# The chunk recurrence of an S5 branch: eight chunks at a time on the DVE, and the context's scan as a tree

## The chip, the cores and the metric

The kernel runs on one core of one Trainium2 chip. The metric is the time of one execution on the device in microseconds (us). The engines are named as in the profile: PE is the matrix engine (PEld its weight loads), DVE the vector engine, ACT the scalar engine, POOL (here also "the Pool") a second vector-like engine, SP the engine that issues the loads from HBM.

## The reference: what is computed

Two layers of a model with 512 latent tokens and 256 context tokens of 1024 features, all in float32. Each layer projects its normed tokens and feeds three mixers side by side, attention, a short convolution and a state space (S5), gates and sums the three, projects, and then runs an MLP:

```python
zx = xn @ w_in
att_x = merge_heads(blocked_attend(q_x, k_all, v_all)) @ w_o
conv_x = short_conv(...)
s5_x, s5_h = s5_branch(zh_s5, zx[..., OFF_S5:OFF_G], a_re, a_im, ...)
y = (g[:, :, 0] * y_att + g[:, :, 1] * y_conv + g[:, :, 2] * y_s5) @ w_out
```

The S5 branch has 32 groups of 64 complex states, in two directions (the latent tokens follow the context in each). For each state it is the recurrence `s[t] = A s[t-1] + B u[t]` over the 768 tokens, and the output is a product of the states with C. The second layer needs the context's outputs no more, only the state at its end.

## The kernel before

The matmuls are exact to float32 in three passes: a block of weights comes by an SP load (tile `wr`), ACT rounds it to `wh` (L175), the DVE subtracts for `wl` (L176; the Pool does it in layer 1's first gate stage, `LOP`), and PE multiplies high by high and high by low (L265) and low by high (L271). A list of steps sets in which order the blocks are emitted, with a look-ahead for the loads and the splits. Other work is put in as a generator: after some of the steps `bg.step()` advances it to its next `yield`. A scheduler that plans the instructions on a time line then decides each engine's final order.

S5 goes by chunks of eight tokens: 32 chunks of the context and 64 latent ones. PE computes each chunk's own contribution to the state at its end (the drive) into the tile `W`, 128 partitions (64 states of two directions) by 2 (real, imaginary), 32 groups and 96 chunks; the chunks are innermost, so the 64 numbers of one chunk lie 384 bytes apart. Then `recur` (L1268) runs `W[s] += A^8 W[s-1]` over the chunks, four TENSOR_TENSORs of 64 elements for each: L1286 and L1288 multiply by the real and the imaginary part of `A^8` (tile `arec`), L1287 and L1289 add. In layer 0 steps 1 to 30 are on the DVE and 31 to 95 on the Pool (`RCUT`); in layer 1, which has the context's end state from elsewhere, the 64 latent steps are on the DVE. Its `yield`s are doled out in the gate stages: `gate` (L1310) multiplies by the gate's weights and ACT takes the sigmoid `sg` (L1314), `merge` (L1320) forms `m` from `sg` and the product (L1324, then L1326 and L1327). The first gate stage (attention's gate) goes with the recurrence; in the second (the convolution's) the readout begins, once the recurrence has been drained: `read_load` copies the states of a quarter of the groups, shifted by a chunk, into `so` (ACT L1385, DVE L1383 and L1386), and `read_mm` multiplies them by a table `ct` (L1401).

In layer 1 the context's 32 chunks are run through by `early_scan` (L1202) during attention, in two halves of 16 groups: 31 steps of four Pool instructions of 32 elements each (L1207 to L1210). Slabs are tiles of 768 numbers a partition, from one ring of 40 that nearly all activations share.

Of the kernel before, what the change touches and what calls it, by code (L numbers as in the profile page):

```python
# [10 lines left out]
F32 = mybir.dt.float32  # L11
# [3 lines left out]
OP = mybir.AluOpType  # L15
# [10 lines left out]
G = 32  # L26
CH = 16
T = 8
# [11 lines left out]
RCUT = (30, 95)  # L40
RSTEP = 6
# [30 lines left out]
def hybrid_kernel(ctx: ExitStack, tc: tile.TileContext, x, c, ctx_in, c_ctx, ada_w, ada_b, norm_mix, w_in,  # L72
# [30 lines left out]
    def load(dst, src):  # L103
        """a load; the first ones go in the order in which they are given."""
        ins = nc.sync.dma_start(dst, src)
        if order[0]:
            tc.keep_in_program_order(ins)
# [55 lines left out]
    class Weights:  # L163
        """A block of weights: loaded, then split into hi and lo."""
# [13 lines left out]
        def cols(self, o, stride, nk):  # L178
            """the k tiles [128, 128] from column o on, hi and lo."""
            return [[w[:, o + k * stride:o + k * stride + 128] for k in range(nk)] for w in (self.hi, self.lo)]  # L180

    def block(src):
        """src [nk * 128, ncol] -> [128, nk, ncol]"""
# [42 lines left out]
    class Background:  # L226
        """Work that is emitted in small steps between the blocks of the main stream."""
# [20 lines left out]
    def staged(items, *stages):  # L248
        """item i goes through stage s in step i + s."""
# [23 lines left out]
    def mm3(ps, w, ah, al, sg, o=0):  # L273
        """ps[:, s:e] = sum_k W[k]^T a[k] with W = wh + wl, a = ah + al."""
# [23 lines left out]
    def ada_mm(i, st):  # L298
        """four column tiles of the array work side by side."""
# [26 lines left out]
    def rsqrt_(ss, n, scale):  # L326
        """returns 1 / sqrt(ss * scale + eps), [128, n] (Newton from an integer estimate)."""
# [10 lines left out]
    def col_stats(acc, s, e, scale):  # L338
        """sums of acc[:, s:e] over partitions -> 1 / rms, tokens on the partitions."""
# [14 lines left out]
    def modulate(l, w, X, rb, segments, xh, xl, ks=range(KD), lag=MLAG):  # L354
        """xn[:, s:e] = rms(x) * norm * (1 + scale) + shift, split; segments: (s, e, which vectors)."""
# [37 lines left out]
    arec = [cst.tile([128, 2, 2, G], F32, name=f"arec{l}") for l in range(2)]  # L393

    def s5_prep(l):
# [4 lines left out]
        def inputs(g8):  # L400
            """B and C of eight groups."""
# [40 lines left out]
        def weave(*chains):  # L442
            """chains of small instructions that don't depend on each other, side by side."""
# [61 lines left out]
        def signs():  # L505
            """sn = s_ * n2 + c_ * u_ with the sign q; cs = c_ * n2 + s_ * u_ with the sign m_."""
# [44 lines left out]
        def factor():  # L551
            """f = (A - 1) / a"""
# [18 lines left out]
        # powers by slot: A^(s + 1) and A^(8 - s) for C, A^s and A^(7 - s) for B (forward, backward)  # L571
# [31 lines left out]
        def tables(u, st):  # L603
            """C A^k and A^k B for two groups."""
# [110 lines left out]
    def kv_part(k):  # L715
        """k tile k of the first two blocks, for all tokens."""
# [30 lines left out]
    def rot_cols(v, o):  # L747
        """columns o..o+32 of v [128, k, n] are pe; the next 32 become rot(pe)."""
# [6 lines left out]
    def roped(d, t):  # L755
        """rows 64-95 of d, lat: pe * cos + rot * sin, with rot in the rows 96-127."""
# [4 lines left out]
    def first_blocks(blocks, SEG, xargs, done):  # L761
        """The first two blocks after a norm: the tokens of SEG[0] go first, while SEG[1] is still being normed.

        xargs: (layer, which norm, the sums); done[i](ps) takes the product of block i."""
# [32 lines left out]
    def layer(l):  # L797
# [68 lines left out]
        # keys' rotary part  # L866
# [24 lines left out]
        # S5 inputs, to [(T - 1 - i, ch), group, chunk]  # L891
# [125 lines left out]
        def scores(h, half, kts):  # L1017
            """exp(s - max) and its sums, 256 queries (which come scaled)."""
# [19 lines left out]
        def turned(kts, P):  # L1038
            """P^T, split: pairs of key tiles side by side."""
# [660 lines left out]
```

## Time and profile before

| | |
|---|---|
| runs | 2454.41, 2459.8, 2459.3 us; median 2459.3 |
| profiled execution | span 2455.2 us |
| busy | PE 96%, DVE 55%, ACT 36%, POOL 21% of the span |
| layer 0: chunk recurrence | on the DVE from 475.4 us, on the Pool to 623.5 |
| layer 0: first readout on PE | 621.9 us |
| layer 1: chunk recurrence | on the DVE, last instruction at 1891.8 us |
| layer 1: first readout on PE | 1896.8 us |

Times are positions in the span of the profiled execution, which is 4.1 us shorter than the median. A line of a group names the code line, the engine, the operation, output and inputs by tile, the shape (partitions x elements) and the count; then busy time and mean duration, then idle time of the engine before these instructions and what ended it. A line of waits says who waited (engine, tile, line) for whom, in total, how often, and the longest.

### The profile page before, as it was taken

What the parts mean: (1) busy time and instruction counts of PE and PEld (TensorE: products, weight loads), DVE (VectorE), ACT (ScalarE), POOL (GpSimd) and SP (SyncE); (2) the same over time, 40 slices, a digit from 0 to 9 for tenths busy, and PEclk for the clock granted to TensorE, in tenths of its full rate; (3) what the DMA queues carried; (4) which work ended last, traced back from release to release, by engine and by line L of the source; (5) the groups of instructions that cost most, each with busy time, mean ns of one, the idle gap of its engine ahead of it and who ended that gap; (6) DMA issues with size and microseconds to landing.
All of it is one profiled execution on the core that took longest, in us unless ns stands there. A gap on an engine that the chain in (4) does not pass through costs nothing. (4 is left out here: it accounts for less than half of the span.)

```text
span 2455.2 us, 36706 instructions
## 1 busy us (share of the span) xinstructions
PE 2364.2 (96%) x14326; PEld 1989.0 (81%) x14326; DVE 1352.6 (55%) x2577; ACT 887.3 (36%) x1520; POOL 516.1 (21%) x906
## 2 busy tenths in 40 slices
PE   5889999999899999999999999999998999999998
PEld 3778888888788888888888888888776788888887
DVE  6985456743322466666533337566678435644455
ACT  5545345412242342332222215455531433432222
POOL 3561111069101110222300001217750010100000
PEclk7999999999999999999999999999998999999999
DMA  9544443421442223455533214333451834333331
GB/s 294 135 115 119 124 133 108 129 87 50 143 143 61 61 85 109 123 149 167 147 120 93 67 54 139 71 97 79 127 160 53 247 99 122 93 95 97 100 96 52
DMA packets 410049, 278.76 MB, mean 114 GB/s; under 512 B 77476, under 2 KB 401236, under 8 KB 409876
## 3 DMA queue, kind: packets, MB, share of 16 engines
q1 hardware_dynamic: 409876, 276.41, 39.2%
q8 instruction: 113, 1.85, 0.3%
q14 instruction: 60, 0.49, 0.1%
HBM read 239.92 MB, written 36.44 MB: 113 GB/s over the span
## 5 line engine op out<-in xcount | busy, mean ns | idle before, releaser
L175 ACT ACTIVATE wh<-wr 128x1024 fp32r<-128x1024 f32 (+1 forms) x294 | 292.7, 999 | 492.8 <-PE psA L271 278.8
L176 DVE TENSOR_TENSOR wl<-wr,wh 128x1024 fp32r<-128x1024 f32 (+1 forms) x281 | 329.4, 1175 | 210.3 <-ACT wh L175 209.0
L265 PE MATMUL psA<-xh,wh 128*128 128x512 f32 (+1 forms) x1312 | 347.0, 342 | 4.9 <-DVE zr L823 3.5
L265 PE MATMUL psA<-xh,wl 128*128 128x256 f32 (+1 forms) x1312 | 344.3, 340 | 0.0
L271 PE MATMUL psA<-xl,wh 128*128 128x256 f32 (+1 forms) x1312 | 243.8, 337 | 0.0
L265 PEld LDWEIGHTS psA<-xh,wh 128*128 128x128 f32 x1312 | 205.4, 190 | 37.3 <-ACT xh L364 3.9
L265 PE MATMUL psB<-xh,wl 128*128 128x512 f32 (+1 forms) x576 | 225.1, 391 | 6.4 <-DVE wl L176 6.4
L265 PE MATMUL psB<-xh,wh 128*128 128x512 f32 (+1 forms) x576 | 225.8, 393 | 3.4 <-ACT sg L1314 2.6
L265 PEld LDWEIGHTS psA<-xh,wl 128*128 128x128 f32 x1312 | 204.8, 190 | 28.8 <-issue 0.4
L271 PEld LDWEIGHTS psA<-xl,wh 128*128 128x128 f32 x1312 | 199.8, 188 | 28.5
L271 PE MATMUL psB<-xl,wh 128*128 128x512 f32 (+1 forms) x576 | 143.3, 388 | 0.0
L1522 DVE SCALAR_TENSOR_TENSOR X<-psA,mod,X 128x512 f32<-128x512 f32 x120 | 68.5, 612 | 132.0 <-PE psA L271 132.0
L265 PEld LDWEIGHTS psB<-xh,wl 128*128 128x128 f32 x576 | 109.2, 190 | 28.9 <-DVE wl L176 7.6
L265 PEld LDWEIGHTS psB<-xh,wh 128*128 128x128 f32 x576 | 109.1, 189 | 27.7 <-ACT sg L1314 3.0
L1522 DVE SCALAR_TENSOR_TENSOR X<-psB,mod,X 128x512 f32<-128x512 f32 (+1 forms) x108 | 70.8, 660 | 99.1 <-PE psB L271 98.6
L271 PEld LDWEIGHTS psB<-xl,wh 128*128 128x128 f32 x576 | 106.6, 188 | 22.2 <-issue 0.9
L265 PE MATMUL psB<-hh,wh 128*128 128x512 f32 (+1 forms) x352 | 123.9, 362 | 0.2 <-DVE X L1522 0.2
L265 PE MATMUL psB<-hh,wl 128*128 128x512 f32 (+1 forms) x352 | 123.6, 360 | 0.0
L265 PE MATMUL psA<-hh,wh 128*128 128x512 f32 x448 | 117.9, 344 | 0.0
L265 PE MATMUL psA<-hh,wl 128*128 128x512 f32 x448 | 115.7, 340 | 0.0
L1483 POOL TENSOR_TENSOR sg<-sg,sg 128x768 f32<-128x768 f32 (+1 forms) x16 | 27.9, 1745 | 329.7 <-ACT sg L1482 329.7
L1592 DVE SCALAR_TENSOR_TENSOR relu<-psA,relu 128x768 f32<-128x768 f32 (+1 forms) x32 | 30.0, 939 | 114.9 <-ACT relu L1591 114.8
(418 smaller groups left out, 4531.2 us busy)
## 6 DMA issues: line engine op xcount, KB each, us to landing
wr<-in_mlp_w_dram SPq DMA_DIRECT2D x128, 512.0 KB, 3.5
wr<-in_w_in_dram SPq DMA_DIRECT2D x88, 512.0 KB, 4.5
wr<-in_ada_w_dram SPq DMA_DIRECT2D x66, 512.0 KB, 5.2
wr<-tab SPq DMA_DIRECT2D x24, 512.0 KB, 4.1
ct<-tab SPq DMA_DIRECT2D x32, 384.0 KB, 4.2
ar<-in_ada_w_dram SPq DMA_DIRECT2D x30, 384.0 KB, 6.6
tab<-s5u SPq DMA_DIRECT2D x32, 256.0 KB, 4.1
tab<-s5v SPq DMA_DIRECT2D x32, 256.0 KB, 2.3
```

What stands on the lines that cost most here:

```text
L175: nc.scalar.activation(self.hi[:, :self.n], self.raw[:, :self.n], AF.Copy)
L176: look.get("lo", nc.vector).tensor_sub(self.lo[:, :self.n], self.raw[:, :self.n], f32(self.hi[:, :self.n]))
L265: nc.tensor.matmul(ps[:, s - o:e - o], w[p][k], ah[k][:, s:e], start=(k == 0 and p == 0), stop=False)
L271: nc.tensor.matmul(ps[:, s - o:e - o], w[0][k], al[k][:, s:e], start=False, stop=(k == n - 1))
L1483: nc.gpsimd.tensor_mul(s[:, :nt], s[:, :nt], s2[:, :nt])
L1522: nc.vector.scalar_tensor_tensor(X[:, ft, s:e], ps, modT[l][:, 8 * w + ft, i:i + 1], X[:, ft, s:e], op0=OP.mult, op1=OP.add)
L1592: nc.vector.scalar_tensor_tensor(r[:, s:e], ps, 0.0, r[:, s:e], op0=OP.max, op1=OP.mult)
```

## The change

The recurrence of a layer is done in four parts, all on the DVE. The chunks are cut into blocks of `LB` = 8 (12 blocks in layer 0, 8 in layer 1). (a) Seven inner steps run the recurrence within all blocks at once, as if each block began from zero: four instructions of 768 elements (layer 0) or 512 (layer 1), whose operands in `W` go from block to block in steps of eight chunks, 32 bytes (L1308 to L1311). (b) 21 small instructions make a table of the powers of `A^8` up to the eighth (L1315 to L1327). (c) A chain carries the state from the end of a block to the end of the next, four instructions of 64 elements each, 11 times in layer 0 and 8 in layer 1 (L1332 to L1335). (d) The fill adds, for each of the seven other positions in a block, the power times the state at the end of the block before: four multiplications and two additions (L1343 to L1347).

The context's scan of layer 1 becomes a tree of five levels on the DVE: at each, pairs of neighbours are joined, 8 instructions of 256, 128, 64, 32 and 16 elements (L1227, L1228) for each half of the groups, with a table of five powers made first. Only the last chunk's state is complete at the end, which is all that is read. Four slabs are new (`rs1` twice, `pw8`, `rc1`), and the second of two output blocks now advances the background work too.

```diff
-RCUT = (30, 95)
-RSTEP = 6
+LB = 8
...
+        def early_powers():
+            L["rc"] = slab("rc1")
+            pw = L["pw"] = L["rc"][:, 256:736].rearrange("p (i k g) -> p i k g", i=5, k=3)
+            t = sm.tile([128, 2, G], F32, name="r1")
+            ve = nc.vector
+            ve.tensor_copy(pw[:, 0, 0], arec[l][:, 0, 0])
+            ve.tensor_copy(pw[:, 0, 2], arec[l][:, 1, 1])
+            for i in range(5):
+                ve.tensor_scalar(pw[:, i, 1], pw[:, i, 2], -1.0, None, op0=OP.mult)
+                if i < 4:
+                    ve.tensor_mul(t[:, 0], pw[:, i, 0], pw[:, i, 0])
+                    ve.tensor_mul(t[:, 1], pw[:, i, 2], pw[:, i, 2])
+                    ve.tensor_sub(pw[:, i + 1, 0], t[:, 0], t[:, 1])
+                    ve.scalar_tensor_tensor(pw[:, i + 1, 2], pw[:, i, 0], 2.0, pw[:, i, 2], op0=OP.mult, op1=OP.mult)
         def early_scan(h):
-            W, a = L["Wc"], arec[l][:, :, :, 16 * h:16 * h + 16]
-            e = nc.gpsimd
-            for s in range(1, NCC):
-                r1, r2 = sm.tile([128, 2, 16], F32, name="r1c"), sm.tile([128, 2, 16], F32, name="r2c")
-                e.tensor_mul(r1, a[:, 0], W[:, :, :, s - 1])
-                e.tensor_add(r1, r1, W[:, :, :, s])
-                e.tensor_mul(r2, a[:, 1], W[:, ::-1, :, s - 1])
-                e.tensor_add(W[:, :, :, s], r1, r2)
-            e.tensor_copy(L["S"][:, :, 16 * h:16 * h + 16], W[:, :, :, NCC - 1])
+            W, ve = L["Wc"], nc.vector
+            for i in range(5):
+                d, n = 1 << i, NCC >> (i + 1)
+                lo_, hi_ = W[:, :, :, d - 1::2 * d], W[:, :, :, 2 * d - 1::2 * d]
+                r = L["rc"][:, 0:16 * n].rearrange("p (g c) -> p g c", g=16)
+                for m in range(2):
+                    for k, x in ((0, lo_[:, m]), (1 + m, lo_[:, 1 - m])):
+                        co = L["pw"][:, i, k, 16 * h:16 * h + 16, None].to_broadcast([128, 16, n])
+                        ve.tensor_mul(r, co, x)
+                        ve.tensor_add(hi_[:, m], hi_[:, m], r)
+            ve.tensor_copy(L["S"][:, :, 16 * h:16 * h + 16], W[:, :, :, NCC - 1])
         def early():
             for i, _ in enumerate(staged(list(range(8)), early_load, early_mm, early_turn)):
+                if i == 2:
+                    early_powers()
...
-            W = E["W"]
-            for s in range(NCC if l else 1, NCHUNK):
-                e = nc.vector if s <= RCUT[l] else nc.gpsimd
-                if s <= RCUT[l] and s % RSTEP == RSTEP - 1:
+            W, A, ve = E["W"], arec[l], nc.vector
+            c0 = NCC if l else 0
+            nb = (NCHUNK - c0) // LB
+            B = W[:, :, :, c0:].rearrange("p m g (b j) -> p m g b j", j=LB)
+            r1, r2 = (slab("rs1")[:, 0:2 * G * nb].rearrange("p (m g b) -> p m g b", m=2, g=G) for _ in range(2))
+            co = [A[:, k, :, :, None].to_broadcast([128, 2, G, nb]) for k in range(2)]
+            for j in range(1, LB):
+                ve.tensor_mul(r1, co[0], B[:, :, :, :, j - 1])
+                ve.tensor_mul(r2, co[1], B[:, ::-1, :, :, j - 1])
+                ve.tensor_add(r1, r1, B[:, :, :, :, j])
+                ve.tensor_add(B[:, :, :, :, j], r1, r2)
+                yield
+            pw = slab("pw8").rearrange("p (j k g) -> p j k g", j=LB, k=3)
+            ve.tensor_copy(pw[:, 0, 0], A[:, 0, 0])
+            ve.tensor_copy(pw[:, 0, 2], A[:, 1, 1])
+            for k in (1, 2, 4):
+                v = [t[:, 0, :, 0:k].rearrange("p g k -> p k g") for t in (r1, r2)]
+                b0, b1 = (pw[:, k - 1, m, None, :].to_broadcast([128, k, G]) for m in (0, 2))
+                x0, x1 = pw[:, 0:k, 0], pw[:, 0:k, 2]
+                ve.tensor_mul(v[0], x0, b0)
+                ve.tensor_mul(v[1], x1, b1)
+                ve.tensor_sub(pw[:, k:2 * k, 0], v[0], v[1])
+                ve.tensor_mul(v[0], x0, b1)
+                ve.tensor_mul(v[1], x1, b0)
+                ve.tensor_add(pw[:, k:2 * k, 2], v[0], v[1])
+            ve.tensor_scalar(pw[:, :, 1], pw[:, :, 2], -1.0, None, op0=OP.mult)
+            b1 = 0 if l else 1
+            for b in range(b1, nb):
+                last, x = W[:, :, :, c0 + b * LB - 1], W[:, :, :, c0 + b * LB + LB - 1]
+                q1, q2 = (sm.tile([128, 2, G], F32, name=n) for n in ("r1", "r2"))
+                ve.tensor_mul(q1, pw[:, LB - 1, 0, None, :].to_broadcast([128, 2, G]), last)
+                ve.tensor_mul(q2, pw[:, LB - 1, 1:3], last[:, ::-1])
+                ve.tensor_add(q1, q1, x)
+                ve.tensor_add(x, q1, q2)
+                if b % 6 == 5:
                     yield
-                r1 = sm.tile([128, 2, G], F32, name="r1")
-                r2 = sm.tile([128, 2, G], F32, name="r2")
-                e.tensor_mul(r1, arec[l][:, 0], W[:, :, :, s - 1])
-                e.tensor_add(r1, r1, W[:, :, :, s])
-                e.tensor_mul(r2, arec[l][:, 1], W[:, ::-1, :, s - 1])
-                e.tensor_add(W[:, :, :, s], r1, r2)
+            n = nb - b1
+            last = W[:, :, :, c0 + b1 * LB - 1:NCHUNK - 1:LB]
+            r1, r2 = r1[:, :, :, 0:n], r2[:, :, :, 0:n]
+            for j in range(LB - 1):
+                for m in range(2):
+                    ve.tensor_mul(r1[:, m], pw[:, j, 0, :, None].to_broadcast([128, G, n]), last[:, m])
+                    ve.tensor_mul(r2[:, m], pw[:, j, 1 + m, :, None].to_broadcast([128, G, n]), last[:, 1 - m])
+                x = B[:, :, :, b1:, j]
+                ve.tensor_add(r1, r1, r2)
+                ve.tensor_add(x, x, r1)
+                if j % 2:
+                    yield
...
-                    step(lambda release: (out_mm(wt, ft, 1), release()), None, True)
+                    step(lambda release: (out_mm(wt, ft, 1), release(), bg.step(L.get("bgn", 1))), None, True)
```

PE around layer 0's first readout (`ct`, `so`, `U`: table, shifted states and inputs; `xh`, `xl`: tokens high and low; `vh`, `vl` the convolution's). Before, it comes after the first three matmuls of a gate block:

```order
L265 MATMUL psA<-xh,wh 128x512
L265 MATMUL psA<-xh,wh 128x256
L265 MATMUL psA<-xh,wl 128x512
L1401 MATMUL psB<-ct,so 64x128 x4
L1401 MATMUL psB<-ct,U 64x128 x2
```

After, behind the last low matmuls of the block before:

```order
L270 MATMUL psA<-xl,wh 128x256
L270 MATMUL psA<-xl,wh 128x512
L270 MATMUL psA<-xl,wh 128x256
L1461 MATMUL psB<-ct,so 64x128 x4
L1461 MATMUL psB<-ct,U 64x128 x2
L1461 MATMUL psB<-ct,so 64x128 x4
L1461 MATMUL psB<-ct,U 64x128 x2
```

The readout has moved ahead by 107 matmuls; the blocks that stood in front of it now follow.

DVE in layer 0's first gate stage, from one merge `m` on (`r` or `rs`: scratch; `arec`: the coefficients). Before:

```order
L1324 TENSOR_TENSOR m<-sg,psA 128x768
L1286 TENSOR_TENSOR r_5220<-arec_120,W 128x64
L1288 TENSOR_TENSOR r_5221<-arec_120,W 128x64
L176 TENSOR_TENSOR wl<-wr,wh 128x1024
L1287 TENSOR_TENSOR r_5220<-r_5220,W 128x64
L1289 TENSOR_TENSOR W<-r_5220,r_5221 128x64
```

After:

```order
L1384 TENSOR_TENSOR m<-sg,psA 128x768
L1308 TENSOR_TENSOR rs_5082<-arec_120,W 128x768
L1309 TENSOR_TENSOR rs_5083<-arec_120,W 128x768
L175 TENSOR_TENSOR wl<-wr,wh 128x1024
L1310 TENSOR_TENSOR rs_5082<-rs_5082,W 128x768
L1311 TENSOR_TENSOR W<-rs_5082,rs_5083 128x768
L1308 TENSOR_TENSOR rs_5082<-arec_120,W 128x768
```

The instructions of a step are as many, but of 768 elements. From this `m` to the next stand eight of them and two `wl`.

DVE in layer 1's first gate stage, from a merge on. Before:

```order
L1324 TENSOR_TENSOR m<-sg,psB 128x512
L1289 TENSOR_TENSOR W<-r_17583,r_17584 128x64
L1286 TENSOR_TENSOR r_17589<-arec_121,W 128x64
L1288 TENSOR_TENSOR r_17590<-arec_121,W 128x64
L1287 TENSOR_TENSOR r_17589<-r_17589,W 128x64
L1289 TENSOR_TENSOR W<-r_17589,r_17590 128x64
```

After:

```order
L1384 TENSOR_TENSOR m<-sg,psB 128x512
L1310 TENSOR_TENSOR rs_16906<-rs_16906,W 128x512
L1311 TENSOR_TENSOR W<-rs_16906,rs_16907 128x64x8
L1308 TENSOR_TENSOR rs_16906<-arec_121,W 128x512
L1309 TENSOR_TENSOR rs_16907<-arec_121,W 128x512
L1310 TENSOR_TENSOR rs_16906<-rs_16906,W 128x512
L1311 TENSOR_TENSOR W<-rs_16906,rs_16907 128x64x8
```

Before, 33 instructions of the recurrence stood between this merge and the next; after, nine.

## Rows read from the trace of the kernel before

**Rows 1.** The page, part 1: busy us (share of the span) xinstructions

```profile
PE 2364.2 (96%) x14326; PEld 1989.0 (81%) x14326; DVE 1352.6 (55%) x2577; ACT 887.3 (36%) x1520; POOL 516.1 (21%) x906
```

**Rows 2.** Windows: us, busy PE, PEld, DVE, ACT, POOL, clock, DMA share, GB/s

```profile
475.00:600.00 125.00, 125.00 (x723) 109.38 (x722) 63.09 (x156) 25.84 (x29) 81.05 (x200) 1.00 0.29 85
616.30:626.40 10.10, 4.46 (x50) 3.69 (x52) 4.50 (x7) 2.07 (x3) 7.18 (x19) 0.50 0.01 3
1625.00:1750.00 125.00, 122.77 (x741) 102.90 (x740) 79.11 (x118) 64.42 (x131) 78.23 (x218) 1.00 0.36 97
1799.00:1890.00 91.00, 78.32 (x328) 63.56 (x326) 86.99 (x268) 18.33 (x23) 21.07 (x9) 0.92 0.28 80
1841.60:1848.40 6.80, 4.29 (x10) 3.46 (x11) 6.36 (x27) 0.00 (x0) 0.21 (x1) 0.50 0.08 30
1865.50:1872.30 6.80, 3.26 (x8) 2.59 (x9) 6.66 (x19) 0.00 (x0) 0.00 (x0) 0.50 0.20 51
1892.80:1896.20 3.40, 3.40 (x9) 2.65 (x8) 0.52 (x1) 0.00 (x0) 0.00 (x0) 0.50 0.45 116
```

**Rows 3.** Waits, layer 0, 600 to 625 us: total, times, longest us

```profile
ACT so L1385 <- POOL W L1289: 14.0, 1, 14.0
...
PE psB L1401 <- ACT so L1385: 10.6, 1, 10.6
```

**Rows 4.** Timeline around layer 0's first readout: start us, us, engine line op

```profile
592.62 0.51 PE L265 MATMUL psA<-vh,wh 128*128 128x512 f32 x2
...
610.99 0.40 PE L265 MATMUL psA<-xh,wl 128*128 128x512 f32 x1
...
621.04 1.56 ACT L1385 ACTIVATE so<-W 64x760 f32<-64x760 f32 x2 [13.99 <-POOL W L1289]
...
621.93 0.91 PE L1401 MATMUL psB<-ct,so 128*64 128x128 f32 x6 [10.55 <-ACT so L1385]
```

**Rows 5.** Timeline, DVE, layer 0: first instructions of two successive serial steps

```profile
475.41 0.27 DVE L1286 TENSOR_TENSOR r<-arec,W 128x64 f32<-128x64 f32 x1
...
476.39 0.28 DVE L1286 TENSOR_TENSOR r<-arec,W 128x64 f32<-128x64 f32 x1
```

**Rows 6.** Groups of instructions by shape, DVE, 475 to 600: busy us, mean ns

```profile
L176 DVE TENSOR_TENSOR wl<-wr,wh 128x1024 fp32r<-128x1024 f32 x15 | 18.9, 1258 | 51.2 <-ACT wh L175 50.9
...
L1324 DVE TENSOR_TENSOR m<-sg,psA 128x768 f32<-128x768 f32 x7 | 6.7, 952 | 4.4 <-PE psA L271 4.3
L280 DVE TENSOR_TENSOR vl<-vr,vh 128x768 fp32r<-128x768 f32 x4 | 4.2, 1100 | 0.0
```

**Rows 7.** Contiguous DVE operands: groups, one line's durations (ns), timeline

```profile
L280 DVE TENSOR_TENSOR wl<-psB,wh 128x512 fp32r<-128x512 f32 x104 | 68.5, 683 | 32.2 <-ACT wh L279 31.6
...
L532 DVE TENSOR_TENSOR s5t<-s5pb,s5e x32: 405/418/958, 49.6 to 1190.4; 128x256 f32<-128x256 f32 x32
...
953.43 0.23 DVE L530 TENSOR_TENSOR s5pw<-s5wk 128x64 f32<-128x64 f32 x1
```

**Rows 8.** ACT lines L306 and L1431: duration ns min/median/max, first and last start

```profile
L306 ACT ACTIVATE ev<-psB x48: 356/383/390, 18.3 to 2087.8; 128x256 f32<-128x256 f32 x48
...
L1431 ACT ACTIVATE ge<-psA x8: 643/708/748, 1945.4 to 1955.5; 128x256 f32<-128x256 f32 x8
```

**Rows 9.** Layer 1's gate stage: PE's waits, and the Pool's low weights

```profile
PE psB L265 <- DVE m L1324: 6.3, 1, 6.3
PE psB L265 <- DVE wl L176: 5.6, 1, 5.6
PE psB L265 <- ACT sg L1314: 2.6, 1, 2.6
...
L176 POOL TENSOR_TENSOR wl<-wr,wh 128x1024 fp32r<-128x1024 f32 x9 | 21.9, 2437 | 27.6 <-ACT wh L175 27.6
```

**Rows 10.** Layer 1's attention: PE's longest wait, and the Pool's recurrence

```profile
PE psA L1029 <- ACT P L1033: 1.6, 3, 1.0
...
L1208 POOL TENSOR_TENSOR r1c<-r1c,wr 128x32 f32<-128x32 f32 x62 | 19.8, 320 | 0.2
```


## The prediction

> **What bounds the kernel now.** I read the page's busy shares first: TensorE (PE) is busy 96% of the span and the DVE 55% [rows 1]. So an edit of DVE and Pool work can only pay where PE waits for it, and only cost where it makes PE wait. I then cut the trace into windows at the three places that the change touches [rows 2], and asked in each which wait ends last.
>
> Layer 0, the gate stage and the first readout: from 475 to 600 PE is busy for all of 125.00 us, the DVE for 63.09, the Pool for 81.05 [rows 2]. The recurrence over the chunks runs there beside the matmuls, 30 steps on the DVE from 475.4, the rest on the Pool. Its end is not hidden: in the list of waits PE stands 10.6 us in front of the readout for the shifted states `so`, and the ACT copy that makes them had waited for the Pool's L1289 [rows 3]. In the timeline PE's last matmul before the wait starts at 610.99, ACT copies at 621.04, PE goes on at 621.93 [rows 4]. The granted clock is 0.50, the lower of its two levels (1.2 of 2.4 GHz), over 616.3 to 626.4 [rows 2], after the wait began; the 50 matmuls there have 4.46 us of busy time, so about 2.3 us are lost on top. The change can win at most 10.55 + 2.3 = 12.85 us here.
>
> Layer 1, the same stage: here the DVE is the bound. From 1799 to 1890 it is busy 86.99 of 91.00 us and PE only 78.32 [rows 2]. PE's waits name it: 6.3 us for the merge `m`, 5.6 for the low weights `wl`, 2.6 for a sigmoid that stood behind the copies of the states [rows 9]. Three stretches of 6.8, 6.8 and 3.4 us run at clock 0.50 [rows 2]. What the DVE gains or loses in this stage goes straight into the time.
>
> Layer 1, attention: from 1625 to 1750 PE is busy 122.77 of 125 us, the DVE 79.11 [rows 2]; PE's one wait of size there is 1.6 us for `P` [rows 10]. The context's recurrence on the Pool (four groups of 62 instructions, 17 to 20 us each [rows 10]) holds nobody up.
>
> **The change, part by part.** Prices first. A DVE TENSOR_TENSOR whose operands are contiguous takes 0.952 us for 768 elements, 0.683 for 512, 0.418 for 256 and 0.23 for 64 [rows 6, 7]; for 352 I read 0.52 between them. One serial step of before, four instructions of 64 elements, takes 0.98 us from start to start (475.41 to 476.39), and one of them lasts 0.27 where the contiguous one lasts 0.23 [rows 5, 7]: an operand that steps through W in strides of 384 bytes costs 0.04 to 0.05 us on 64 elements.
>
> The new inner steps read and write W in strides of 32 bytes, 768 or 512 elements an instruction. The trace of before has no DVE instruction like that, and this price decides the case. Let x be the extra time per stepping element. Lower end: x = 0, if the 0.05 is paid once per instruction (0 is also the floor: a strided operand has no row in which it is quicker). By the 64-element rows, if it is paid per element: 0.053/64 = 0.83 ns. ACT, writing 256 elements in 32-byte steps, takes 0.708 us where a contiguous write takes 0.383 [rows 8]: 1.3 ns per element, on another engine, and my upper end. I take 0.83 for an instruction that only reads W in steps (the nearest row) and 1.3 for one that writes W so (the only row of such a write).
>
> The Trainium skill, "Vector Engine (DVE) Microarchitecture Reference", section 5.2 (Measured stream behaviour on trn2), speaks against the change: a stream runs at full rate only in runs of two or more adjacent 4-byte words; one source that hops at every element takes 1.73 ns per column against 1.05, and a destination alone in steps of 24 words 2.50. An estimate from that page is 0.69 extra for reads and 1.46 for writes, which would end at about 2473; no row of before tests it.
>
> Layer 0. Removed: 30 DVE steps, 65 Pool steps and the wait above. Added on the DVE at x = 0: inner steps 7 x (4 x 0.957 - 0.12 overlap) = 26.0 us; table of powers, 21 small instructions of about 0.22, 4.6; chain over 11 blocks at the old step's 0.98, 10.8; fill 7 x (4 x 0.52 + 2 x 0.89 - 0.2) = 25.6. Sum 67.0. In its queue before the last of them stand 12 `wl` (1.258), 9 merges (0.952) and 4 `vl` (1.100) [rows 6], 28.1 less 0.04 overlap each, 27. From 475.4 the states are complete at 569.4. Stepping elements: 21 x 768 reads and 7 x 768 writes in the inner steps, 28 x 352 reads and 7 x 704 writes in the fill, 36,288 in all; at my prices 13.4 + 7.0 + 8.2 + 6.4 = 35.0, so 604.4, and with 1.3 for the copies the readout may start at 605.7. PE gets to it sooner than before: the instruction order puts the first readout 107 matmuls earlier, right behind a block's last `xl,wh`, which in before's trace is 592.62 [rows 4]. So PE waits 13.1, loses another 2.3 to the clock, and loses none of the old 12.85: net **+2.5 us**. The DVE has then 129 us of work in 129: `wl` and merges are late within that same wait, not beyond it.
>
> Layer 1. Before: 64 x 0.98 = 63 us. After at x = 0: inner 18.5 (28 of 512), table 4.6, chain of 8 blocks 7.9, fill 20.0 (28 of 256 at 0.418, 14 of 512), 51.0: 12 less. Stepping elements 25,088: 10,752 reads and 3,584 writes, then 7,168 and 3,584; 8.9 + 4.7 + 5.9 + 4.7 = 24.2. Net **+12.2 us**, all of it on the path, since PE waits for this queue already. What else is in the queue stays: merges, `wl`, `vl`, and the stretch that the Pool's nine `wl` of 2.437 us [rows 9] put on DVE instructions beside them.
>
> Attention. The Pool loses some 74 us. The DVE gains the tree, 16 instructions at each of five sizes: 0.418 us for 256 elements [rows 7], 0.29, 0.23, 0.18 and 0.17 read off for 128 down to 16, 20.6 us, and 7,936 stepping elements at 0.83, 6.6; with 22 powers at 0.2 and the gaps at ten levels about 33. It has 46 idle of 125 [rows 2], so I book **+2** for reduces of the scores that come later behind a burst of eight, with bounds -4 (the DVE free of a busy Pool beside it) and +10 (rival 3).
>
> The one more `bg.step` per two out blocks moves DVE work and the drive's loads on SP earlier, which is in the order used above. Four new slabs out of a ring of 40 can hold back a load in SP's queue and the loads behind it; the windows' DMA shares of 0.29 to 0.36 [rows 2] leave room to catch up, so I book 0, at most 2.
>
> Sum: 2.5 + 12.2 + 2 = +16.7. The profiled execution has a span of 2455.2, 4.1 under the median 2459.3, so the sum is put on the median: **2476 us**.
>
> **Rivals.** (1) *The extra is paid per instruction* (x near 0): a 768-element inner step stays near 1.0 us. Then the states are ready at 569 + 1.3, before PE asks: -12.85, layer 1 -12, attention +2: about 2436. For it: the only DVE evidence of a stride cost is 0.05 on short instructions. Against: the ACT rows, where the loss on 256 elements is far above 0.05.
> (2) *Gain and loss cancel.* With one x for reads and writes the change is 61.4 x - 42.5, zero at x = 0.69, an inner instruction of 1.48 us; from 0.61 to 0.77 it is within 5 us of before. About 2460. For it: 0.69 lies in the middle of my bounds, 0 and 1.3. Against: only a narrow stretch of x does it.
> (3) *The tree makes the DVE the bound of layer 1's attention* (slower side): 79 + 33 = 112 of 125 us at x = 0.83, 116 at 1.3. The reduce of scores then stands behind bursts of eight instructions, 3 to 5 us, at ten levels, and PE waits about 1 us at each, as its longest wait for `P` does now: +10 in place of +2, 2484 with the rest. It decides once the DVE is some 95% busy there. Against: its 46 us of idle time, and that the reduces need not stand behind a whole burst.
>
> **How the numbers follow.** Forecast 0.52, (1) 0.17, (2) 0.15, (3) 0.13, something else 0.03. A difference under 0.2% (5 us) is what measurements of this kernel cannot tell from none. The forecast alone spans 2467 (x = 0.83 throughout, +8) to 2497 (1.3 throughout, +37). The lower end for 8 in 10 is x = 0.35: layer 0 fully hidden at -12.85, layer 1 -3, attention +2, so 2446; the upper, 2504, is 1.3 throughout with rival 3's +8 on top. Faster: (1) and the low edge of (2), 0.20; the same: 0.15; slower: the forecast, (3) and the rest, 0.65.
>
> **What would show it.** In the profile after, L1308 to L1311 of 768 elements should last 1.6 to 1.9 us and those of 512 1.1 to 1.3; near 0.95 and 0.69 the forecast falls and rival 1 holds. The last fill instruction of layer 0 should end near 604, with PE waiting about 13 us for `so` again, at an earlier place, and a half clock after it; if PE does not wait there, the layer 0 term is wrong by up to 15. In layer 1 the last fill should end some 12 us later than 1890 did, with longer waits of PE for `m` and `wl`. In layer 1's attention the DVE should be 90% busy with PE's waits for `P` below 4 us; above 8, rival 3.

## The result, and the profile after

| | before | changed | ratio |
|---|---|---|---|
| median of the runs, us | 2457.91 | 2475.57 | 1.0069, 95% interval 1.0057 to 1.0081 |
| span of the profiled execution, us | 2455.2 | 2472.1 | |
| busy: PE, DVE, Pool, us | 2364.2, 1352.6, 516.1 | 2371.5, 1460.0, 346.1 | |

The change costs 17.7 us between the medians, 17.0 (14 to 20) by the ratio; +16.7 and 2476 were forecast. The line numbers of the changed kernel are lower by 1 than those of before up to L1197, and its recurrence is L1308 to L1347.

Layer 0 first. The DVE's groups from 470 to 620 us (count, then busy us and mean ns) show the price that the case hung on: 768 elements in steps of 32 bytes take 1.69 us, 352 take 0.85, 704 take 1.61.

```profile
L1311 DVE TENSOR_TENSOR W<-rs,rs 128x768 f32<-128x768 f32 x7 | 11.9, 1696 | 0.2
L1308 DVE TENSOR_TENSOR rs<-arec,W 128x768 f32<-128x768 f32 x7 | 11.8, 1690 | 0.1
...
L1344 DVE TENSOR_TENSOR rs<-pw,W 128x352 f32<-128x352 f32 x14 | 11.4, 854 | 0.0
...
L1347 DVE TENSOR_TENSOR W<-W,rs 128x704 f32<-128x704 f32 x7 | 11.3, 1612 | 0.1
```

The windows of the changed kernel (columns as in [rows 2]) have the DVE at 122 of 125 us in that stage, where it had 63; in layer 1's attention it is at 102, where it had 79. The two middle rows are stretches of layer 0 at the lower clock, 0.50.

```profile
475.00:600.00 125.00, 116.45 (x635) 100.16 (x634) 122.14 (x163) 22.09 (x25) 0.22 (x2) 0.95 0.26 75
520.70:527.50 6.80, 3.41 (x11) 2.93 (x12) 6.80 (x6) 0.00 (x0) 0.00 (x0) 0.50 0.43 111
578.70:585.50 6.80, 5.71 (x18) 4.87 (x19) 6.80 (x9) 1.76 (x2) 0.00 (x0) 0.50 0.09 25
1625.00:1750.00 125.00, 120.27 (x725) 100.68 (x724) 101.98 (x213) 63.52 (x131) 21.91 (x32) 1.00 0.33 88
```

In PE's waits from 470 to 660 us the wait for the shifted states is gone [rows 3]; in its place PE stands twice, 8.5 us in all, for a merge.

```profile
PE psA L264 <- DVE m L1384: 8.5, 2, 5.4
```

The timeline of the DVE around the first of these waits shows how a merge comes late. PE stood still from about 518.7 to 524.1 us. Its next block needs the buffer that `m` at 523.08 sets free, and before it in the queue stand two inner instructions and a `wl`.

```profile
514.20 1.72 DVE L1311 TENSOR_TENSOR W<-rs,rs 128x768 f32<-128x768 f32 x1
...
519.13 1.54 DVE L1310 TENSOR_TENSOR rs<-rs,W 128x768 f32<-128x768 f32 x1
...
521.72 1.53 DVE L1311 TENSOR_TENSOR W<-rs,rs 128x768 f32<-128x768 f32 x1
523.08 0.95 DVE L1384 TENSOR_TENSOR m<-sg,psA 128x768 f32<-128x768 f32 x1
```

One more thing is in these rows: L1311 took 1.53 us while PE stood still and 1.72 beside running matmuls.

The last fill instruction of layer 0 starts at 600.2 us and the states are complete at 601.8 (forecast: 604.4). PE comes to the readout at 607.9 and need not wait there.

PE runs the same matmuls in the same order in both traces up to before's 592.6 us, and again from its 717.4 on. So the lag of the changed kernel can be counted matmul by matmul, against the same count at the first sigmoid of the gates. At 592.6 it is 15.3 us: 8.5 in the two waits, some 4.5 in the stretches at clock 0.50 behind them (half of their 9.1 us of busy PE), and 2.3 in matmuls that go a little slower. At 717 it is 1.6, for here PE doesn't pay what it paid before: 10.6 us for `so`, 0.7 for a load of `ct` and 2.3 to the clock, 13.6 in all. So the waits and their half clocks cost layer 0 no more than the old one, 13.0 against 13.6. At 840 the lag is 3.9: another 2.2 us have gone with no wait and at full clock. The sigmoids `sg` of the last third of layer 0's mixers show it, before and after; eight of them, the last one 91.6 and 93.3 us behind the first:

```profile
L1482 ACT ACTIVATE sg<-psA x8: 812/812/813, 734.4 to 826.0; 128x768 f32<-128x768 f32 x8
...
L1542 ACT ACTIVATE sg<-psA x8: 812/812/813, 736.2 to 829.5; 128x768 f32<-128x768 f32 x8
```

What the slower matmuls may be due to is taken up below, under the one more background step.

Layer 1's gate stage, PE's waits from 1790 to 1960 us: the same three as in [rows 9], the first two longer by 5.4 and 3.5 us.

```profile
PE psB L264 <- DVE m L1384: 11.7, 2, 9.5
PE psB L264 <- DVE wl L175: 9.1, 1, 9.1
PE psB L264 <- ACT sg L1374: 2.5, 1, 2.5
```

The seven adds of the fill on the DVE, 1795 to 1912 us, as a group and by their spread (duration ns min/median/max, first and last start):

```profile
L1347 DVE TENSOR_TENSOR W<-W,rs 128x512 f32<-128x512 f32 x7 | 7.7, 1100 | 0.2
```

```profile
L1347 DVE TENSOR_TENSOR W<-W,rs x7: 1083/1094/1142, 1873.3 to 1906.0; 128x512 f32<-128x512 f32 x7
```

The states are complete at 1907.1, 17.0 us later than in before's trace, where the copy of the states began at 1890.1; 7.6 of these 17 were there when the stage began (first merge at 1792.5 against 1784.9).

Layer 1's attention, PE's waits from 1600 to 1810 us:

```profile
PE psB L264 <- DVE vt L975: 1.9, 1, 1.9
PE psA L1028 <- ACT P L1032: 1.6, 4, 0.8
PE psB L1057 <- DVE wl L279: 1.5, 2, 1.0
...
PE psB L1044 <- DVE cy L932: 0.9, 1, 0.9
```

`P` is waited for as before [rows 10]. New are `vt`, `wl` and `cy`, pieces of other work that the DVE does between the units, 4.3 us in all where before had 0.5 for `vt` and `wl`.

Read along the trace, the changed kernel is 0.1 us ahead at the first sigmoid of the gates (452.4 against 452.5), 1.8 behind at the last third of layer 0's mixers (736.2 against 734.4), 3.8 behind at layer 0's first residual, 7.6 at layer 1's first merge, 16.9 at the end. The residual's row (first start 843.9; 840.1 before):

```profile
L1582 DVE SCALAR_TENSOR_TENSOR X<-psA,mod,X x120: 469/608/753, 843.9 to 1444.3; 128x512 f32<-128x512 f32 x60, 128x256 f32<-128x256 f32 x60
```

### The profile page after: what moved, and what is told of

Read it like the earlier page. It is cut to its first block, busy times and chain, and to the rows that moved or that the text cites. A ratio compares the mean times of both kernels' runs of the same rounds, so it can differ in the third digit from the quotient of the medians.

```text
span 2472.1 us, 36196 instructions
## 1 busy us (share of the span) xinstructions
PE 2371.5 (96%) x14326; PEld 1991.3 (81%) x14326; DVE 1460.0 (59%) x2564; ACT 895.9 (36%) x1526; POOL 346.1 (14%) x396
## 5 line engine op out<-in xcount | busy, mean ns | idle before, releaser
L270 PE MATMUL psA<-hl,wh 128*128 128x512 f32 x448 | 88.2, 339 | 0.0
```

The costliest lines, as they stand in the source:

```text
L270: nc.tensor.matmul(ps[:, s - o:e - o], w[0][k], al[k][:, s:e], start=False, stop=(k == n - 1))
```

## The experiments

The changed kernel with the code of before put back part by part gives the terms one by one. A flag for each layer and one for the scan choose the old code, in all three as in this core; the one more background step goes with a layer's blocks:

```diff
+            if not BLK[l]:
+                for s in range(NCC if l else 1, NCHUNK): ...   # the serial steps of before
+                return
...
+            if not TREE: ...                                   # the serial scan of before, on the Pool
...
-   release(), bg.step(L.get("bgn", 1))
+   release(), BLK[l] and bg.step(L.get("bgn", 1))
```

**Layer 0 alone** (`BLK = (1, 0)`, no tree).

> The blocks of eight only in layer 0; layer 1's recurrence and the context's scan as before. The theory (three separate terms; layer 0's wait moves from the readout to the merges of the gate stage) expects the time of before +3 to +5 us: the trace after is 3.8 us behind at layer 0's first MLP update (843.9 against 840.1). The rival, that the three parts disturb each other through the shared slabs and the order, expects something else than the +3.8, by 3 us or more.

Measured: 2462.98 against 2458.57, ratio 1.0022 (1.0013 to 1.0031): +3 to +8 us, which doesn't shut out the upper side of the rival. The trace has the 3.9 us of the changed kernel: from the first sigmoid of the gates to the first residual it takes 391.5 us as that one does, before's 387.6. (In other traces with before's code in layer 0 it is 386.7 to 389.6.) PE's waits from 470 to 660 us are the changed kernel's, with no wait for `so`:

```profile
PE psA L268 <- DVE m L1412: 9.2, 2, 5.3
```

**Layer 1's recurrence alone** (`BLK = (0, 1)`, no tree).

> The blocks of eight only in layer 1's recurrence. The theory (DVE-bound stage, 24 us of strides against 12 us saved) expects +9 to +10 us over before, the amount by which the trace after falls back between layer 1's first merge (+7.6) and its end (+16.9). The rival, that part of those 9 us comes from the attention before it or from slabs, expects under +6.

Measured: 2467.06, ratio 1.0032 (1.0020 to 1.0045): +5 to +11 us, middle 7.9; the interval doesn't shut out the rival's under 6, but the trace takes 9.1 us more than before's from layer 1's first merge to its end. PE's waits from 1780 to 1920 us repeat those of the changed kernel, so nothing from attention or the other layer is needed for them:

```profile
PE psB L268 <- DVE m L1412: 11.7, 2, 9.4
PE psB L268 <- DVE wl L179: 9.1, 1, 9.1
```

**The tree alone** (`BLK = (0, 0)`).

> Only the context's scan of layer 1 as a tree on the DVE, both recurrences as before. The theory expects +2 to +4 us: the trace after loses 3.3 us between the end of layer 0's MLP (+4.3) and layer 1's first merge (+7.6). The rival, that these 3 us are the late drive or slabs of the blocked recurrence, expects within 1 us of before. That the tree is the bound of attention expects +8 or more.

Measured: 2462.46, ratio 1.0015 (1.0006 to 1.0024): +1.5 to +5.9, middle 3.7. PE's waits from 1600 to 1790 us are the changed kernel's; the first of them:

```profile
PE psB L268 <- DVE vt L979: 1.9, 1, 1.9
```

The three middles add to 17.0 us, as the ratio 1.0069 does (17.0). The runs give no sign that the parts disturb each other, though each middle is good only to 2 or 3 us.

**The same instructions over adjacent numbers.**

```diff
-            B = W[:, :, :, c0:].rearrange("p m g (b j) -> p m g b j", j=LB)
+            B = W[:, :, :, c0:].rearrange("p m g (j b) -> p m g b j", j=LB)
...
-                last, x = W[:, :, :, c0 + b * LB - 1], W[:, :, :, c0 + b * LB + LB - 1]
+                last, x = B[:, :, :, max(b - 1, 0), LB - 1], B[:, :, :, b, LB - 1]
...
-            last = W[:, :, :, c0 + b1 * LB - 1:NCHUNK - 1:LB]
+            last = B[:, :, :, 0:n, LB - 1]
```

> The changed kernel with the same instructions in the same number, but the inner steps, the chain and the fill read and write W as if the blocks lay side by side (runs of 12 or 8 adjacent numbers in place of steps of 32 bytes); the chunks are not stored in that order, so the states that come out are of the wrong chunks. The theory (the price is paid for stepping elements) expects the 768-element steps at about 1.0 us in place of 1.69, no wait of PE at the merges of layer 0, and 2437 to 2445 us, faster than before by 12 to 20. The rival (the price is the number of instructions, the chain or the queue's order) expects within 5 us of the changed kernel, 2470 to 2480.

Measured: 2438.43, ratio to before 0.9922 (0.9908 to 0.9935), that is 36 us under the changed kernel (0.9922 / 1.0069). Groups from 470 to 620 us, the window of the stage, and the first readout's row (start 591.8):

```profile
L1311 DVE TENSOR_TENSOR W<-rs,rs 128x768 f32<-128x768 f32 x7 | 6.7, 956 | 0.2
L1308 DVE TENSOR_TENSOR rs<-arec,W 128x768 f32<-128x768 f32 x7 | 6.7, 955 | 0.1
```

```profile
475.00:600.00 125.00, 125.00 (x774) 108.86 (x772) 98.36 (x174) 28.44 (x34) 1.00 (x6) 1.00 0.32 92
```

```profile
L1461 PE MATMUL psB<-ct,so x192: 272/273/324, 591.8 to 635.6; 128*64 128x128 f32 x96, 128*32 128x128 f32 x96
```

PE has no wait from 470 to 660 us. With as many instructions, chain and table included, and only the steps taken away, the loss turns into a gain; the rival falls. This is also rival 1 of the prediction as it would have been: 2436 was worked out for it.

**A list of prices.**

```diff
+    Y = big.tile([128, 6144], F32, name="Y", tag="X")
+    for _ in range(REP):
+        v.tensor_mul(qa[:, 0:n], qb[:, 0:n], Y[:, 0:8 * n:8])       # and so on, one line for each form
```

> The kernel before, with a list of DVE TENSOR_TENSORs put behind its last work, six of each: 256 elements with one source in steps of 4, 8, 16, 32, 64 and 96 bytes, in pairs of adjacent words, then the destination in steps of 32 bytes, then both; 64 elements in steps of 4, 32 and 384 bytes; 768 and 512 elements in steps of 32 bytes; runs of 8 adjacent elements; a broadcast source. The theory (a price per element) expects 256 elements to go from 0.42 to 0.62 to 0.70 us once the step is over 4 bytes, 768 to 1.5 to 1.7, 64 to 0.27, and no extra for pairs, for runs of 8 or for the broadcast. The rival (a price per instruction) expects 0.05 more at every size. A price that grows with the step would show between 8 and 96 bytes.

A single run, of which only the list is read. In order: 256 elements with one source in steps of 4, 8, 16, 32 and 96 bytes, in pairs; destination in steps of 32; destination and one source; 64 in steps of 32; 768 and 512 in steps of 32; 512 in runs of 8:

```profile
L1676 DVE TENSOR_TENSOR qa<-qb,Y x6: 424/425/426, 2454.8 to 2457.1; 128x256 f32<-128x256 f32 x6
...
L1678 DVE TENSOR_TENSOR qa<-qb,Y x6: 410/426/426, 2457.5 to 2462.1; 128x256 f32<-128x256 f32 x6
...
L1680 DVE TENSOR_TENSOR qa<-qb,Y x6: 607/609/611, 2462.6 to 2465.8; 128x256 f32<-128x256 f32 x6
...
L1682 DVE TENSOR_TENSOR qa<-qb,Y x6: 617/618/619, 2466.4 to 2469.7; 128x256 f32<-128x256 f32 x6
...
L1686 DVE TENSOR_TENSOR qa<-qb,Y x6: 792/792/796, 2474.1 to 2478.2; 128x256 f32<-128x256 f32 x6
...
L1688 DVE TENSOR_TENSOR qa<-qb,Y x6: 424/425/426, 2479.0 to 2481.3; 128x256 f32<-128x256 f32 x6
...
L1690 DVE TENSOR_TENSOR Y<-qb,qa x6: 617/618/621, 2481.8 to 2485.1; 128x256 f32<-128x256 f32 x6
...
L1692 DVE TENSOR_TENSOR Y<-Y,qa x6: 617/618/619, 2485.7 to 2489.0; 128x256 f32<-128x256 f32 x6
...
L1696 DVE TENSOR_TENSOR qa<-qb,Y x6: 272/272/273, 2491.2 to 2492.7; 128x64 f32<-128x64 f32 x6
...
L1702 DVE TENSOR_TENSOR qa<-qb,Y x6: 1537/1540/1541, 2500.8 to 2508.6; 128x768 f32<-128x768 f32 x6
...
L1706 DVE TENSOR_TENSOR qa<-qb,Y x6: 1077/1078/1080, 2519.7 to 2525.2; 128x512 f32<-128x512 f32 x6
...
L1708 DVE TENSOR_TENSOR qa<-qb,Y x6: 691/692/693, 2526.3 to 2530.0; 128x512 f32<-128x512 f32 x6
```

The price is per element: (1.540 - 0.958) / 768 = 0.76 ns, (1.078 - 0.692) / 512 = 0.75, (0.618 - 0.425) / 256 = 0.75, 0.958 and 0.692 being the adjacent 768 and the runs of 8. Reads and writes cost the same, both together no more. Steps of 8 bytes, pairs and runs of 8 cost nothing, against what I had expected of the 8 bytes; 96 bytes cost twice as much (0.792). A broadcast source is free too (0.959 for 768).

The Trainium skill, "Vector Engine (DVE) Microarchitecture Reference", section 5.2 (Measured stream behaviour on trn2), has 1.73 to 1.76 ns per column for sources that step at each element and 1.71 for such a destination. Here (1.540 - 0.618) / 512 = 1.80, at 32 bytes and for a source or a destination alike, is near that. The Trainium skill's 2.50 there, which the estimate in the prediction used for a destination, is for steps of 24 words, 96 bytes; it is not reached at 32 bytes, and at 96 the list tried a source alone ((0.792 - 0.425) / 256 = 1.43 ns more than adjacent numbers). The Trainium skill's rule of adjacent words there, as the prediction told it, doesn't hold here for one source in steps of 8 bytes, which runs at full rate (0.426 against 0.425).

**Prices beside matmuls.** The same three forms (768 adjacent, 768 and 512 in steps of 32 bytes), five of each with PE idle and ten beside a run of matmuls:

```diff
+            for i in range(140):
+                for s_, e_ in ((0, 512), (512, 768)):
+                    nc.tensor.matmul(ps[:, s_:e_], wq[:, 128 * (i % 6):128 * (i % 6) + 128], xq[:, s_:e_], ...)
```

> The kernel before with, behind its last work, DVE TENSOR_TENSORs of 768 elements (adjacent, then one source in steps of 32 bytes) and of 512 (steps of 32 bytes), first with PE idle and then beside a run of 280 matmuls of 512 and 256 columns. In layer 0 of the changed kernel the stepping instruction takes 1.53 us while PE stands still and 1.69 to 1.75 beside matmuls. The theory (PE's reading of the same memory stretches an instruction that steps, not one that reads adjacent numbers) expects 1.54 alone and 1.65 to 1.75 beside the matmuls for 768, 1.08 and 1.12 to 1.2 for 512, and 0.96 in both cases for adjacent numbers. The rival (the stretch comes from the weights' loads or from ACT) expects 1.54 in both.

A single run again. Duration in ns, min/median/max, of the fifteen of each form:

```profile
L1680 DVE TENSOR_TENSOR qa<-qb,Y x15: 946/959/959, 2453.9 to 2499.6; 128x768 f32<-128x768 f32 x15
...
L1682 DVE TENSOR_TENSOR qa<-qb,Y x15: 1537/1699/1699, 2459.8 to 2507.5; 128x768 f32<-128x768 f32 x15
...
L1684 DVE TENSOR_TENSOR qa<-qb,Y x15: 1077/1178/1191, 2467.7 to 2514.1; 128x512 f32<-128x512 f32 x15
```

The timeline of the DVE has the low values first, with PE idle, and then five in 8.62 us beside it:

```profile
2462.94 1.54 DVE L1682 TENSOR_TENSOR qa<-qb,Y 128x768 f32<-128x768 f32 x1
...
2480.86 8.62 DVE L1682 TENSOR_TENSOR qa<-qb,Y 128x768 f32<-128x768 f32 x5
```

So 1.54 becomes 1.70 beside running matmuls, 1.08 becomes 1.18, and adjacent numbers keep their 0.96. That is layer 0's 1.69. In layer 1 the undisturbed instructions of 512 took 1.08 to 1.11, less than the 1.18 here; why they are stretched less is open.

**The one more background step.** In layer 0 a difference was left that no wait explains: from 750 to 800 us PE is busy throughout in both traces, but gets through 291 matmuls before and 285 after, in the same order. The window of before:

```profile
750.00:800.00 50.00, 50.00 (x291) 44.07 (x289) 12.82 (x12) 10.91 (x12) 5.54 (x3) 1.00 0.22 64
```

Two runs look for it. Three slabs more in layer 0's recurrence:

```diff
+                if l == 0:
+                    for nm in ("rs1", "rs1", "pw8"):
+                        nc.vector.memset(slab(nm)[:, 0:8], 0.0)
```

> The kernel before with three slabs more taken in layer 0's recurrence, each written once and not used: it moves the later slabs to the places that they have in the changed kernel, and nothing else. From 660 to 840 us the matmuls of 512 columns go every 235 ns in each kernel with blocks in layer 0, every 230 to 232 ns in the kernels without. If the places of the slabs set that, the matmuls of this kernel go every 235 ns there and the time is 2 to 3 us above before; if the order does, they stay at 230 to 232 ns and the time within 1 us.

Measured: 2459.33 against 2459.55, ratio 0.9998 (0.9987 to 1.0008), 291 matmuls in that window. This shift of the slabs doesn't do it. The kernel before with the one more `bg.step` in layer 0 only:

> The kernel before with only the one more step of background work per two output blocks in layer 0, recurrences and scan as before: the readout then stands 11 rows earlier in PE's order in place of 107. If that step's changed order is what makes the matmuls of 512 columns go every 235 ns in place of 230 from 660 to 840 us, they do so here and the time is 1 to 3 us above before; if the rate comes with the blocks themselves (their early readout), they stay at 230 to 232 and the time within 1 us.

Measured: 2464.02 against 2458.29, ratio 1.0023 (1.0013 to 1.0034): +3 to +8 us, more than expected and as much as layer 0's whole part of the change. The same window, and PE's waits from 470 to 700 us:

```profile
750.00:800.00 50.00, 50.00 (x285) 43.31 (x284) 12.82 (x12) 10.91 (x12) 5.51 (x3) 1.00 0.22 64
```

```profile
PE psB L1489 <- ACT so L1473: 11.5, 1, 11.5
PE psB L1489 <- DMA ct<-tab: 1.4, 1, 1.4
```

In the trace the way from the first sigmoid of the gates to the first residual is 6.9 us longer than before's. Counted matmul by matmul, 1.6 are the two waits (0.9 more for `so` than in [rows 3], and 1.4 for a load of `ct` in place of 0.7), 2.2 are lost after 717 us as in the changed kernel, and 2.5 by 606 us, ahead of both waits, where PE's order is still before's; 0.6 is left.

The slower matmuls after 717 us go with the step: in all 14 traces of this case the stretch from the first sigmoid of the mixers' last third to the first residual lasts 107.6 us where layer 0 has the step (seven) and 105.6 where it has not (seven). But that the order of the work makes them slower is not shown. The trace of the list of prices is before's kernel up to the list, and from 500 to 580 us it too gets through fewer matmuls than before's trace, in the same order, with PE busy throughout:

```profile
500.00:580.00 80.00, 80.00 (x463) 70.00 (x462) 31.01 (x61) 16.68 (x19) 62.70 (x157) 1.00 0.32 94
...
500.00:580.00 80.00, 80.00 (x455) 69.37 (x454) 31.32 (x62) 16.70 (x19) 62.40 (x155) 1.00 0.32 96
```

What sets the rate is open. Open too is how much of layer 0's part the step makes by itself: the blocks without it were not run over this layout of W.

**W stored block beside block.** The drive's evictions read PSUM in steps and write W at position j * blocks + b, the shifted copies read it back in steps, and layer 1 takes the context's state in at its first chunk; the scan is the serial one:

```diff
+                wp = wv.rearrange("p g (j b) -> p g j b", j=LB)
+                turn = lambda a: a.rearrange("p g (b j) -> p g j b", j=LB)
-                nc.scalar.activation(wv[0:64], pv[0:64], AF.Copy)
+                nc.scalar.activation(wp[0:64], turn(pv[0:64]), AF.Copy)
...
+            cp(fw[:, :, :, 1:], bv[0:64, :, :, 0:LB - 1])
+            cp(fw[:, :, 1:, 0], bv[0:64, :, 0:-1, LB - 1])
```

> The blocks of eight with W really stored block beside block (position j * blocks + b), so that the inner steps and the fill run over adjacent numbers: the evictions of the drive read PSUM in steps and write adjacent, the shifted copies of the readout read W in steps, layer 1 takes the context's state in at its first chunk by one more step of four instructions; the context's scan is the serial one on the Pool. The theory expects the time of the contiguous run (2438) less the tree's 4 us, plus up to 2 us for the first shifted copy and the steps: 2433 to 2440. The rival, that the reordering costs what it saves on ACT and the DVE's copies, expects 2448 or more.

Measured: 2436.64 against 2457.95, ratio 0.9912 (0.9890 to 0.9934). Three variants of it followed.

> As the relaid kernel, but with the context's scan as the tree on the DVE. The theory, that the tree costs by itself some 4 us in layer 1's attention, expects 2 to 5 us over the relaid kernel; the rival, that it only cost because the drive behind it was late, expects within 1 us of it.

Measured: 2440.76, ratio 0.9928 (0.9912 to 0.9945). The middle is 4 us over, as expected, but the intervals overlap. In the traces the way from the first residual to layer 1's first merge is 952.0 us against the relaid kernel's 948.2, the same 4.

> As the relaid kernel, with the low weights of layer 1's first gate stage on the DVE (13 of 1.24 us) in place of the Pool, whose instructions stretch the DVE ones beside them. If that stretch (some 18 us before) is still on the path, 3 to 8 us less than the relaid kernel; if the DVE is no more the bound there, within 2 us of it.

Measured: 2440.74, ratio 0.9933 (0.9913 to 0.9953): no gain is seen, though neither expectation is met and the intervals overlap. In its trace PE waits only 0.8 us for `wl` in this stage, 7.0 in the relaid kernel's, but 2.3 for ACT's `wh`, 2.2 for `sg` and 1.8 for `W` in its place. The edit also puts the 13 low weights on the DVE, so what the Pool's stretch alone costs there is not shown.

> The relaid kernel (e6) without the one more background step per two output blocks in layer 0; layer 1 keeps it. If that step costs by itself, as the run before says, the matmuls of 512 columns go every 230 to 232 ns again from 700 to 840 us and the time is 2 to 4 us under the relaid kernel (2436.6), 2432 to 2435; if its cost there is outweighed by the earlier readout, 2436 or more.

Measured: 2434.84 against 2457.46, ratio 0.9909 (0.9895 to 0.9924), the fastest median, though not to be told from the relaid kernel's. The matmuls are back at 290 in that window, and PE's waits in layer 1's gate stage, 1770 to 1900 us, are at 8 us as in the relaid kernel:

```profile
750.00:800.00 50.00, 50.00 (x290) 44.10 (x289) 14.10 (x14) 11.48 (x13) 7.39 (x4) 1.00 0.22 64
```

```profile
PE psB L268 <- DVE wl L179: 7.0, 1, 7.0
PE psB L268 <- DVE m L1423: 1.1, 1, 1.1
```

It beats both kernels: some 22 us under before and 39 under the change as it was made (0.9909 / 1.0069).

## Why the prediction was right

*The price x of a stepping element.* It decided the sign, and 0.83 from the 64-element rows was nearly right: 0.76 with PE idle, about 0.95 beside matmuls in layer 0 ((1.69 - 0.957) / 768), 0.8 in layer 1 ((1.100 - 0.69) / 512). The second value, 1.3 for writes, taken from ACT, was wrong: the DVE pays the same for both. The two ACT rows behind it also differ in more than the step, for L306 copies and L1431 takes a Gelu. In layer 0 the two errors cancelled (35.0 us forecast; 36,288 elements at 0.95 are 34.5), in layer 1 they did not (24.2 against 25,088 at 0.8, 20.1).

*Layer 0, +2.5.* The trace loses 3.9 by the first residual, the run of it alone 5.4 (3 to 8). The states came when they were forecast, at 601.8 for 604.4, but the path was another. I had PE wait 13.1 us at the readout, with `wl` and merges late "within that same wait". With the DVE at 122 of 125 us, merges that come every 12 us were late themselves; PE paid for two of them, and came to the readout late enough to find it ready. The price of the waits was near all the same, 13.0 us against the old 13.6, where 13.1 + 2.3 against 12.85 was forecast, so they cost nothing net. That PE reached the readout 15.3 us after 592.62, where 15.4 was worked out, is chance. By the prediction's own sign, no wait at the readout, this term was to be wrong by up to 15 us; it was not, for PE had paid elsewhere. What the traces lose in layer 0 is in matmuls that went 2% slower, 2.3 us by 592 and 2.2 after 717. The sum has no term for that, and the second part goes with the `bg.step` that I booked at 0 (at most 2), which costs by itself about as much as the whole of layer 0's part.

*Layer 1, +12.2.* Measured +9.3 in the trace (16.9 - 7.6) and +7.9 (5 to 11) alone. The mechanism was right, all of it on the path and paid at `m` and `wl`; the term was oversized by the 1.3. With the 20.1 us of the measured price it is +8.1.

*Attention, +2.* The tree costs 3.7 (1.5 to 5.9), within the bounds of -4 to +10. Its instructions sum to 28.4 us, 27.2 forecast. What PE waits for was wrong: not the softmax's `P`, but conversions between the units. And the DVE, which was to be 90% busy there, was at 102 of 125 us.

*The sum.* That it came out within 1 us is partly luck: by the runs of one part each, layer 0 and attention cost 2.9 and 1.7 us more than booked, and layer 1 4.3 less.

*The rivals.* Rival 1 (price per instruction) falls by the list of prices. Rival 2 needed x = 0.69: in layer 1 and 0 it was 0.8 and 0.95, close enough that a forecast of "slower" at 0.65 was no more certain than it should have been. Rival 3 expected 112 to 116 us of DVE and +10; it was 102 and 4.

## What to carry to other kernels

Before instructions are made fewer and larger, look at the step of their operands: in layer 1 the four parts come to 51 us at the prices of adjacent numbers, where the serial steps take 63, and to 71 with the measured price of 32-byte steps. The same loops over a tile laid out for them turned 17 us of loss into some 18 of gain, and into 22 with the serial scan and without layer 0's background step. When a queue has as much work as the stage is long, look for the loss at the small results that stand in it every few us, not at the large result at its end. And an edit that only doles work out sooner is an edit: time it alone. Where two traces run the same instructions in the same order, count the lag between them instruction by instruction: it shows where the time went, and here it was not where the waits had moved to.

## What the runs showed of the hardware

- On the DVE 4-byte numbers in steps of 8 bytes are read as quickly as adjacent ones (0.426 and 0.425 us for 256); steps of 16 and 32 bytes cost 0.18 and 0.19 us more, of 96 bytes 0.37 more.
- Running matmuls stretch a stepping DVE instruction by a tenth (1.54 to 1.70 us for 768) and leave one over adjacent numbers as it is (0.96).
- Between traces, the same matmuls in the same order went some 2% slower over 50 to 80 us of uninterrupted work at full clock (463 and 455 matmuls from 500 to 580 us in two traces of one kernel's code; 291 and 285 from 750 to 800 in two kernels); the cause is open.
